# A list scheduler that orders the queues by another model of time

## Chip, cores and metric

One Trainium2 chip, one core. The metric is the device time of one execution in microseconds (us); below, a "run" is one such time, and a profile is one more execution taken with the hardware profiler.

## The reference, cut to what matters

The input `x` is 256 tokens by 1024 columns in float32 and passes through three layers. Layers 0 and 1 have a mixer, a cross-attention into 256 memory tokens and a gated feed-forward part; layer 2 has three mixers side by side, gates over them, and a gated feed-forward part with a short convolution.

```
for layer in range(2):
    y = mlstm_mixer(rms_norm(x, g[0])) if layer == 0 else stick_breaking_mixer(...)
    x = x + rms_norm(y, g[1])
    x = x + rms_norm(memory_cross_attention(rms_norm(x, g[2]), mem_n, ...), g[3])
    x = x + rms_norm(swiglu_ffn(rms_norm(x, g[4]), ...), g[5])
h = rms_norm(x); z = h @ w_in
merged = gate0 * (hgrn2(z) @ w_a) + gate1 * (fox(z) @ w_b) + gate2 * (memory(z) @ w_c)
x = x + merged @ w_out
x = x + conv_glu_ffn(rms_norm(x))
```

All weights are read once from HBM in float32: about 220 MB.

## The kernel before

**How the work is cut.** The tokens are two halves of 128 rows. Every large product splits both operands into a high and a low part of type `fp32r` and adds three products (high by high, high by low, low by high). A weight block of 128 rows x 1024 columns (512 KB) is loaded by a DMA on SP's queue (`load`, line 201), rounded to its high part on ScalarE (`split_weight`, line 209), and the low part is made on VectorE (line 210). Five buffers hold raw blocks, ten hold each of the split parts. The products are in `prod` (lines 238, 239 and 242, with up to 512 columns) and, where the result is wanted transposed, in `project_T` (lines 303 to 305, 256 columns). Two pools of four PSUM banks each take the results.

**The chains beside the products.** Between two stages stand chains of short operations. A norm is: squares summed on ScalarE (line 381), two tiny operations of GpSimd for the power -1/2 (`rstd`, lines 375 and 376), a scaling, transposes on TensorE (line 329), and splits on ScalarE and VectorE (lines 428 and 435). The first projection's chain scales by that factor on ScalarE (line 581) and copies after the transposes (line 356). The mixers have such chains too: attention, softmax and, in layer 2, the decay levels of `hgrn_levels` (lines 1147 to 1173; products at line 363) and the head norms (line 358).

**What sets the order.** Two programs order the work, one after the other.

1. While the kernel is traced, `Net` writes the instructions down in one order. The products are steps; a chain is a generator that yields the microseconds it is to wait, on a clock that advances with the products (0.2135 us for a 512-column product). The weights' loads and splits are written 24 and 14.85 us of that clock ahead of their product.
2. When the trace is closed, a list scheduler walks a model of the machine in time and puts the instructions into each engine's queue. Where an engine can take another instruction, it gets the one that stands earliest in the written order among those whose operands and buffers the model says are ready at that time. So the written order holds except where the model finds the next instruction not ready and a later one ready. Buffers are handed out in the same walk. On the chip each queue runs in the order so fixed and waits on semaphores.

```
def pe(self, us, main=False):          # the clock of the written order
    self.now += us
    if main: self.main += us; self.feed(); self.poll()
...
LEAD = 14.85
LEAD_DMA = 24.0
...
def ahead(self):
    return self.tc.high_priority(offset=60)
```

A few things the scheduler may not change: the first instructions of ScalarE, VectorE and TensorE are in a `manual_schedule` block (`start`), and table loads and some early transfers are pinned behind what was written before them on their engine (`keep_in_program_order`). All other transfers, the small constants and the gain rows (`gain`, line 215) may be moved.

## Time and profile before

| | |
|---|---|
| median of 3 runs | 1330.41 us (1330.31 to 1331.91) |
| profiled execution, its own time | 1330.58 us |
| its span, first to last instruction | 1328.9 us |
| around the span | 1.7 us |
| TensorE matmul busy | 1311.2 us, 8475 instructions |
| VectorE, ScalarE, GpSimd busy | 814.7, 693.1, 125.2 us |
| mean granted TensorE clock | 0.999 |

TensorE's busy time counts from a matmul's start to its modelled end, and neighbours overlap, so 99% busy does not by itself say that nothing can be gained between two products; what it does show is every stretch in which TensorE had no matmul at all. A wait is put down to the instruction whose semaphore came last.

### The profile page before, as it was taken

Reading aid. Unit: us, or ns where it says so; the run is one execution under the profiler, and the core shown is the slowest. Engines: PE = TensorE matmul, PEld = TensorE weight load, DVE = VectorE, ACT = ScalarE, POOL = GpSimd, SP = SyncE. Lnnn points to the kernel's source line nnn. Section 1 sums busy time; section 2 is a strip of 40 time slices with the busy share of each in tenths; the row PEclk is TensorE's granted clock in tenths of the full one; section 3 lists DMA queues with packets and bytes.
Section 4 is the critical chain, followed back from the end, with each engine's and each line's share of the span. In section 5 each row is a group of like instructions: output and inputs, shape, how many; then the busy total and the mean of one; then the engine's idle time right before and its main releaser. Section 6 shows DMA issues by size and latency. Waiting matters only on the chain.

```text
span 1328.9 us, 21515 instructions
## 1 busy us (share of the span) xinstructions
PE 1311.2 (99%) x8475; PEld 1180.9 (89%) x8475; DVE 814.7 (61%) x1229; ACT 693.1 (52%) x1128; POOL 125.2 (9%) x224
## 2 busy tenths in 40 slices
PE   8999999999999999999999999998999999999998
PEld 6889888899998999888889999888998999899997
DVE  6674576745446466468584454677786666766552
ACT  6864565534446577466474344555444534745441
POOL 3000000000001000016210000013224020000000
PEclk9999999999999999999999999999999999999999
DMA  7854562755556533554365655555244356456550
GB/s 254 288 185 133 160 205 84 235 173 170 183 187 204 193 128 127 190 182 139 110 219 167 211 181 179 182 170 163 72 140 127 128 160 207 152 180 197 181 178 32
DMA packets 121438, 224.47 MB, mean 169 GB/s; under 512 B 7448, under 2 KB 19066, under 8 KB 121338
## 3 DMA queue, kind: packets, MB, share of 16 engines
q1 hardware_dynamic: 121338, 223.11, 52.4%
q8 instruction: 66, 1.08, 0.3%
q14 instruction: 34, 0.28, 0.1%
HBM read 222.03 MB, written 1.05 MB: 168 GB/s over the span
## 4 chain that ended last, share of the span: by engine, by line
PE 78%; issue 14%; DVE 2%; POOL 2%; ACT 2%; DMA 1%; SPq 0%; DVEq 0%; POOLq 0%; ACTq 0%
PE mm L242 11%; PE mm L239 11%; PE mm L238 11%; PE tr L305 8%; PE tr L304 8%; PE tr L303 8%; PE tr L363 4%; PE mm L303 3%; PE mm L304 3%; PE mm L305 3%; PE tr L329 3%; PE tr L242 2%; PE tr L239 2%; PE tr L238 2%; DVE lo L210 1%
## 5 line engine op out<-in xcount | busy, mean ns | idle before, releaser
L210 DVE TENSOR_TENSOR lo<-raw,hi 128x1024 fp32r<-128x1024 f32 (+1 forms) x414 | 497.4, 1225 | 269.3 <-ACT hi L209 262.5
L209 ACT CAST hi<-raw 128x1024 fp32r<-128x1024 f32 (+1 forms) x414 | 419.6, 1042 | 202.5 <-PE mm L242 84.5
L238 PE MATMUL mm<-hi,t 128*128 128x512 f32 (+2 forms) x856 | 330.3, 387 | 0.0
L239 PE MATMUL mm<-lo,t 128*128 128x512 f32 (+2 forms) x856 | 327.6, 384 | 0.0
L242 PE MATMUL mm<-hi,t 128*128 128x512 f32 (+2 forms) x856 | 266.3, 386 | 0.0
L303 PE MATMUL tr<-t,hi 128*128 128x256 f32 x864 | 244.7, 283 | 0.0
L305 PE MATMUL tr<-t,lo 128*128 128x256 f32 x864 | 244.6, 283 | 0.0
L304 PE MATMUL tr<-t,hi 128*128 128x256 f32 x864 | 244.5, 283 | 0.0
L239 PEld LDWEIGHTS mm<-lo,t 128*128 128x128 f32 x856 | 161.6, 189 | 30.0
L238 PEld LDWEIGHTS mm<-hi,t 128*128 128x128 f32 x856 | 161.6, 189 | 29.2 <-issue 0.3
L242 PEld LDWEIGHTS mm<-hi,t 128*128 128x128 f32 x856 | 159.1, 189 | 30.2
L303 PEld LDWEIGHTS tr<-t,hi 128*128 128x128 f32 x864 | 165.8, 192 | 0.6
L304 PEld LDWEIGHTS tr<-t,hi 128*128 128x128 f32 x864 | 165.8, 192 | 0.6
L305 PEld LDWEIGHTS tr<-t,lo 128*128 128x128 f32 x864 | 165.8, 192 | 0.0
L303 PE MATMUL mm<-t,hi 128*128 128x256 f32 x576 | 165.7, 288 | 0.0
L304 PE MATMUL mm<-t,hi 128*128 128x256 f32 x576 | 163.0, 283 | 0.0
L305 PE MATMUL mm<-t,lo 128*128 128x256 f32 x576 | 163.0, 283 | 0.0
L303 PEld LDWEIGHTS mm<-t,hi 128*128 128x128 f32 x576 | 110.3, 191 | 2.0 <-issue 0.5
L304 PEld LDWEIGHTS mm<-t,hi 128*128 128x128 f32 x576 | 110.3, 192 | 0.8
L305 PEld LDWEIGHTS mm<-t,lo 128*128 128x128 f32 x576 | 110.2, 191 | 0.0
L375 POOL TENSOR_SCALAR s<-s 128x1 f32<-128x1 f32 x32 | 23.2, 726 | 798.2 <-ACT junk L381 787.1
L363 PE MATMUL tr<-t,t 128*128 128x128 f32 (+4 forms) x672 | 82.1, 292 | 2.9 <-DVE t L1155 2.9
(241 smaller groups left out, 1196.4 us busy)
## 6 DMA issues: line engine op xcount, KB each, us to landing
raw<-in_ffn_w_gate_up SPq DMA_DIRECT2D x88, 512.0 KB
raw<-in_ffn_w_down SPq DMA_DIRECT2D x66, 512.0 KB
raw<-in_w_in SPq DMA_DIRECT2D x54, 512.0 KB
raw<-in_ffn_w_up SPq DMA_DIRECT2D x44, 512.0 KB
raw<-in_xa_w_kv SPq DMA_DIRECT2D x32, 512.0 KB
raw<-in_sb_w_qkv SPq DMA_DIRECT2D x24, 512.0 KB
raw<-in_ml_w_in SPq DMA_DIRECT2D x22, 512.0 KB
raw<-in_xa_w_q SPq DMA_DIRECT2D x16, 512.0 KB
```

The lines of the kernel that those rows point to most:

```text
L209: self.nc.scalar.copy(hi, raw)
L210: self.nc.vector.tensor_sub(lo, raw, hi.bitcast(F32))
L238: nc.tensor.matmul(out, lhsT=a, rhs=wh, start=first and k == 0, stop=False)
L239: nc.tensor.matmul(out, lhsT=a, rhs=wl, start=False, stop=False)
L242: nc.tensor.matmul(out, lhsT=b, rhs=hl[k][0], start=False, stop=last and k == nk - 1)
L303: self.nc.tensor.matmul(out, lhsT=wh, rhs=xh, start=k == 0, stop=False)
L304: self.nc.tensor.matmul(out, lhsT=wh, rhs=xl, start=False, stop=False)
L305: self.nc.tensor.matmul(out, lhsT=wl, rhs=xh, start=False, stop=k == kt - 1)
L329: self.nc.tensor.transpose(ps[:, i * P : (i + 1) * P], src(i), self.ident)
L363: self.nc.tensor.matmul(out, lhsT=lhsT, rhs=rhs, start=start, stop=stop, **kw)
L375: nc.gpsimd.tensor_scalar(e, a, EPS, b, ALU.add, ALU.add)
```

## The change

Before the framework is imported, an environment variable is set that makes the list scheduler walk its second model of time, which keeps one timeline for each engine and queue, in place of its default model. Nothing else is changed: the written order, the instructions, the buffers and the pinned parts are the same. What can differ is the order in each queue, which buffer a tile gets, and with these the waits.

```
+import os
+os.environ["CONCOURSE_TILE_TIMELINE_SIM"] = "all"
 from collections import deque
 
 import concourse.bass as bass
```

## Rows read from the trace of the kernel before

**Rows 1.** The page: span, and busy time of each engine, share, instructions.

```profile
span 1328.9 us, 21515 instructions
...
PE 1311.2 (99%) x8475; PEld 1180.9 (89%) x8475; DVE 814.7 (61%) x1229; ACT 693.1 (52%) x1128; POOL 125.2 (9%) x224
```

**Rows 2.** Waits of TensorE: line waited for, total us, times, longest; ten rows.

```profile
PE tr L363 <- DVE t L1155: 2.9, 3, 1.5
PE tr L329 <- ACT t L581: 2.7, 1, 2.7
PE tr L329 <- DVE t L358: 2.6, 2, 1.7
PE tr L1565 <- DVE mhalf L490: 1.2, 1, 1.2
PE tr L329 <- DMA x<-in_x: 1.1, 1, 1.1
...
PE tr L329 <- DVE t L1221: 0.3, 1, 0.3
```

**Rows 3.** Timeline of the end: start us, us taken, engine, line, operation.

```profile
1323.74 0.39 PE L238 MATMUL mm<-hi,t 128*128 128x512 f32 x1
1323.97 0.39 PE L239 MATMUL mm<-lo,t 128*128 128x512 f32 x1
...
1324.20 0.61 PE L242 MATMUL mm<-hi,t 128*128 128x512 f32 x2
1324.85 0.75 DVE L1696 TENSOR_TENSOR x<-x,mm 128x256 f32<-128x256 f32 x2 [1.97 <-PE mm L242]
```

**Rows 4.** Timeline of the first chain; in brackets the wait and what ended it.

```profile
19.60 5.57 POOL L375 TENSOR_SCALAR s<-s 128x1 f32<-128x1 f32 x1 [15.59 <-ACT junk L381]
...
19.75 5.25 DVE L210 TENSOR_TENSOR lo<-raw,hi 128x1024 fp32r<-128x1024 f32 x5
...
25.85 0.69 ACT L581 ACTIVATE t<-mm,s 128x512 f32<-128x512 f32 x1 [2.71 <-POOL s L376]
...
26.59 0.66 PE L329 MATMUL tr<-ident,t 128*128 128x128 f32 x4 [2.66 <-ACT t L581]
```

**Rows 5.** Stretches: length, busy of PE, PEld, DVE, ACT, POOL, clock, DMA share, GB/s.

```profile
24.00:28.00 4.00, 1.41 (x9) 1.24 (x10) 1.00 (x2) 1.80 (x4) 2.58 (x4) 0.98 0.96 261
28.00:32.00 4.00, 4.00 (x14) 3.00 (x13) 3.88 (x8) 2.20 (x4) 0.00 (x0) 0.59 0.90 267
```

**Rows 6.** Timeline of TensorE in the mixers of layer 2.

```profile
928.97 0.41 PE L363 MATMUL tr<-t,t 128*128 128x64 f32 x2 [1.53 <-DVE t L1155]
929.18 0.37 PE L303 MATMUL mm<-t,hi 128*128 128x256 f32 x1
929.39 0.28 PE L304 MATMUL mm<-t,hi 128*128 128x256 f32 x1
```

**Rows 7.** That stretch, TensorE alone: length, busy, clock, DMA share, GB/s.

```profile
904.00:940.00 36.00, 29.63 (x228) 1.00 0.47 147
```

**Rows 8.** Waits of ScalarE, as in rows 2.

```profile
ACT hi L209 <- PE mm L242: 84.5, 95, 4.9
ACT hi L209 <- PE tr L304: 59.8, 29, 2.9
```

**Rows 9.** Waits of SP's queue, the one that issues the transfers, as in rows 2.

```profile
SPq L201 <- DVE lo L210: 987.6, 356, 22.8
```

**Rows 10.** Timeline of SP's queue: when two transfers were issued.

```profile
6.59 0.34 SPq L1387 DMA_DIRECT2D foxb<-in_fox_f_bias  x1
...
59.74 0.45 SPq L215 DMA_DIRECT2D g<-in_norm_gains  x1
```

**Rows 11.** Line 375 alone: duration min/median/max in ns, first and last start.

```profile
L375 POOL TENSOR_SCALAR s<-s x32: 293/378/5567, 19.6 to 1139.5; 128x1 f32<-128x1 f32 x32
```

**Rows 12.** Transfers: destination, source, queue, operation, count, size of each.

```profile
g<-in_norm_gains SPq DMA_DIRECT2D x6, 512.0 KB
```

## The prediction

> **What bounds the kernel now.** I read the page's busy times first. TensorE has a matmul in 1311.2 of 1328.9 us; VectorE, ScalarE and GpSimd are busy for 61%, 52% and 9% [rows 1]. No other engine is near being the bound, so what an order can change is TensorE's idle time, 1328.9 - 1311.2 = 17.7 us, and the pace of its products.
>
> The list of TensorE's waits comes next. Its ten rows add up to 13.3 us [rows 2]. The end adds 1328.9 - (1324.20 + 0.61) = 4.1 us after the last product, for the last sum and its way out [rows 3]. Together 17.4 of the 17.7 us. Of the 13.3, the waits for `mhalf` (1.2) and for `x` (1.1) lie in the pinned start; 13.3 - 2.3 = 11.0 us are waits that another order could move.
>
> They have two main places. In the first chain (timeline), GpSimd's line 375 began at 19.60 and took 5.57 us, while VectorE ran five splits of line 210 in 5.25 us; ScalarE then waited 2.71 us for the factor and TensorE 2.66 us for ScalarE [rows 4]. The stretches around show what such a wait leaves behind: TensorE was busy for 1.41 of the 4 us to 28, and in the next 4 us the granted clock was 0.59, between its two levels of 1.2 and 2.4 GHz [rows 5]. At full clock the work of those 4 us takes 4 x 0.59 = 2.4, so 1.6 us more were lost, and this late chain cost 2.7 + 1.6 = 4.3 us. The second place is the mixers of layer 2: 36 - 29.63 = 6.4 us without a matmul in 904 to 940 [rows 7]. There a level's small product waits 1.53 us for VectorE's line 1155, and gate products (lines 303 and 304) run right after it [rows 6]; they needed nothing that came in the meantime, so they could have gone first.
>
> The products themselves stand close: two of 512 columns start 0.23 us apart [rows 3]. The order of a queue doesn't change that pace, so nothing is taken from it.
>
> The waits of the other queues show what covers them. ScalarE stood at a split (line 209) 84.5 us in 95 waits and 59.8 in 29 until TensorE had freed a buffer, 4.9 us at the longest [rows 8]; SP's transfers waited 987.6 us for buffers [rows 9]. Weights are thus made as fast as TensorE uses them; outside the start neither transfers nor splits are short.
>
> **The change, part by part.** No instruction is added or taken away: the 1311.2 us of matmuls stay, and the variable itself is read on the host, at no device time. What moves is where the scheduler departs from the written order. That it does so freely today is seen on SP's queue: the bias `foxb`, written in layer 1 far behind the first stages, was issued at 6.59 us, and the first gain row of line 215 shown here at 59.74 [rows 10]. The trace doesn't show the second model's order, so I bound it from the rows.
>
> *Gains.* At most the 11.0 us of movable waits and the 1.6 us of low clock behind the first chain: 12.6 us, a time of 1318.0. At least nothing. I take half of the mixers' 6.4 us, 3.2: a model that keeps a timeline for each queue can find line 1155 late and take the gate products first, but then the chain's later steps stand behind whole groups of products. The middle is a choice between the two ends, since neither row is nearer.
>
> *Losses.* A stage entry is where products need the result of a chain: seven norm chains end in one (four behind the attention outputs, two behind layers 0 and 1's feed-forward part, one behind `w_out`). In the order of today TensorE's waits at all seven together are under 2 us (13.3 - 2.3 - 2.7 - 6.4 = 1.9). A chain that comes late there costs what the first chain cost, 4.3 us: nothing is queued behind the waiting transposes on TensorE that could run, and the splits of VectorE and ScalarE stop too when the buffers are full [rows 8]. Bounds: none late, 0; all seven, 30.1 us. How likely is one? Line 375 ran 32 times with a median of 378 ns and one of 5567 [rows 11]: 1 in 32 met a run of splits, and hurt. A new order moves the splits against all 32. I take two late chains, 8.6 us: nearer to today's one than to seven.
>
> The Trainium skill has a rule on this collision (SBUF — State Buffer, Who interferes with whom): a VectorE instruction with both inputs in SBUF and a GpSimd instruction that reads SBUF lock each other out, for the length of one instruction. Line 210 and line 375 are such a pair, and the row agrees that GpSimd waits. Where they differ is the length: one split of the row is 5.25 / 5 = 1.05 us, and the row shows a whole run of 5.57. By the row two late chains cost 8.6 us; by the rule 2 x 1.05 = 2.1, which is the rival "short collisions" below.
>
> *Nothing.* Table loads, constants and the end stay in the same number; ScalarE's idle half covers them [rows 1].
>
> Sum against the profiled execution's own time: 1330.6 (its span and 1.7 us around it) + 8.6 - 3.2 = 1336.0. The median of the runs is 1330.4, 0.2 us below, so the sum stands for the median as well.
>
> **The rivals.**
>
> *The mixers' waits go (faster).* The second model places the gate products in front of the late level products, and the chains stay in time: 1330.6 - 6.4 = 1324.2; with the first chain mended too, 1318.0 to 1320. For it: ready work stood right behind the waits [rows 6]. Against it: VectorE is the slow one there, and a level that is put off makes the next one late. It decides as long as fewer than two chains (8.6 us) turn late.
>
> *Short collisions, or nearly the same order (same).* The written order and the buffers are unchanged, and today's departures leave TensorE 13.3 us of waits in 8475 instructions. With two collisions of one split each: 1330.6 + 2.1 - 3.2 = 1329.5.
>
> *The variable isn't read (same).* The identical program, 1330.4. The queues would be the same instruction by instruction.
>
> *Transfers in front of the start (slower).* In 24 to 32 us DMA is busy for 0.96 and 0.90 of the time at 261 to 267 GB/s [rows 5]. A gain row of 512 KB [rows 12] takes 2.0 us of that. Both gain buffers filled there would hold the weights back 4.0 us, and with 1.6 us of low clock the time is 1336.2. Against it: SP waits mostly for buffers later on, and the memory's rows are pinned.
>
> *Chains behind waiting splits (much slower).* If the new order puts chain operations on ScalarE behind splits that wait for TensorE, each half of the seven entries can be late by the longest such wait, 4.9 us [rows 8]: 14 x 4.9 = 69 us, 1399. It decides only if the second model frees split buffers much earlier than the chip does.
>
> **How the numbers follow.** Likeliest, two or so late chains against half of the mixers' waits: 0.40, with a range of its own from 1333.3 to 1361. Mixers' waits go: 0.30. Short collisions or nearly the same order: 0.14. Not read: 0.04. Transfers in front: 0.06. Chains behind splits: 0.06. A measurement of this kernel can tell about 0.2%, 2.7 us, from no change. Slower by more: 0.40 + 0.06 + 0.06 = 0.52; within: 0.18; faster: 0.30. The time is the likeliest's, 1336. The range goes from the case in which all movable waits go, 1318, to the one with seven late chains, 1330.6 + 30.1 = 1361; it leaves out the 0.06 of 1399 and about as much again on either end.
>
> **What would show it.** Right: the same 8475 TensorE instructions and about 1311 us of products; TensorE's waits rise by some 5 us, in two or three new rows at transposes of line 329 or products behind a norm, each with a GpSimd line 375 of several us or a late ScalarE step ahead of it and a stretch with the clock under 1.00 after it; the stretch of the mixers loses about half of its 6.4 us. Wrong: TensorE's waits fall to the pinned start and little more (the faster rival); new waits of TensorE for weights in the first 50 us (transfers); the split's waits on ScalarE standing ahead of chain steps at every entry (much slower); or a changed pace of back-to-back products, which none of the cases holds.

## The result: 3.2% slower, and the profile after

The kernel with the second model takes 1374.19 us (median of 4 runs, 1372.44 to 1375.65) against 1330.63 us before on the same chip: ratio 1.0323, 95% interval 1.0310 to 1.0336. I had said 1336 us, at most 1361. The sign was right by luck: the mechanism that I had put into the sum is not the one that made the loss, and the size was not right either.

All line numbers of the kernel after are higher by 2 than those of before (line 329 is 331, line 375 is 377).

The page of the kernel after, to be read against [rows 1]:

```profile
span 1370.7 us, 21546 instructions
...
PE 1326.9 (97%) x8475; PEld 1191.0 (87%) x8475; DVE 812.3 (59%) x1229; ACT 695.0 (51%) x1131; POOL 121.2 (9%) x224
```

The same 8475 matmuls. TensorE is idle for 1370.7 - 1326.9 = 43.8 us in place of 17.7, which is 26.1 us of the 41.8 by which the span grew; the other 15.7 are matmuls that took longer. The mean granted clock, 0.991 in place of 0.999, accounts for most of these: 0.009 of 1370.7 us is about 12 us lost at the low level, against some 1 to 2 before. What made the rest of the 15.7, some 5 us, isn't traced here.

The instructions are not quite the same, though I had said so: ScalarE has 1131 in place of 1128. The three more are loads of a function table, 17 in place of 14, of 1.28 us each, and all three stand between 42 and 60 us. What such loads can do is seen in the last of the experiments.

TensorE's waits after, to be read against [rows 2] (line waited for, total us, times, longest):

```profile
PE tr L999 <- DVE t L993: 4.6, 3, 2.4
PE tr L331 <- ACT t L792: 3.9, 1, 3.9
PE tr L240 <- ACT t L430: 3.1, 4, 1.8
...
PE tr L331 <- DVE t L1223: 2.9, 1, 2.9
PE tr L331 <- DVE t L775: 2.7, 2, 1.7
PE mm L305 <- DVE t L1223: 2.4, 1, 2.4
PE tr L999 <- DVE t L994: 2.4, 1, 2.4
```

There is no single big wait. The head of the list holds steps of quite different chains (attention, head norm, gates), each a few us. Where do they stand? The order of TensorE's queue differs from before's only inside stretches: between them both queues have issued the same set of instructions, so the n-th large product (lines 238 to 242 and 303 to 305) can be compared in the two traces. Nearly all of the loss lies in three stretches (39.4 of the 41.8 us). They are, with the same work, 155.0 to 251.0 us (before 158.5 to 243.7: the cross-attention of layer 0), 470.7 to 573.8 (before 463.0 to 550.9: the stick-breaking attention), and 606.1 to 689.5 (before 583.0 to 653.0: the head norm behind that attention, and what follows). The windows of after, TensorE alone (length, busy, clock, DMA share, GB/s):

```profile
155.00:251.00 96.00, 87.02 (x442) 1.00 0.43 143
470.70:573.80 103.10, 95.03 (x712) 0.97 0.39 124
606.10:689.50 83.40, 73.04 (x366) 0.94 0.42 137
```

and of before:

```profile
158.50:243.70 85.20, 85.20 (x440) 1.00 0.50 161
463.00:550.90 87.90, 87.90 (x713) 1.00 0.43 138
583.00:653.00 70.00, 68.55 (x369) 1.00 0.51 159
```

The same number of matmuls to within three. Before, TensorE was idle for 0, 0 and 1.45 us there; after, for 8.98, 8.07 and 10.36. The three stretches grew by 10.8 + 15.2 + 13.4 = 39.4 us, of which 26.0 are idle time. These stages had next to no wait in the list of before, and I had not looked inside them.

Two stretches answer to rows that I had used. In the first chain, GpSimd's line 377 now takes 1.01 and 1.82 us where it took 5.57 [rows 4], and TensorE is busy without a gap where it was busy for 1.41 of 4 us [rows 5]. The timeline of GpSimd and the windows:

```profile
20.13 1.01 POOL L377 TENSOR_SCALAR s<-s 128x1 f32<-128x1 f32 x1 [16.09 <-ACT junk L383]
...
23.78 1.82 POOL L377 TENSOR_SCALAR s<-s 128x1 f32<-128x1 f32 x1 [2.00 <-ACT junk L383]
```

```profile
24.00:28.00 4.00, 4.00 (x19) 3.30 (x19) 2.91 (x5) 2.05 (x4) 2.15 (x2) 1.00 0.84 199
28.00:32.00 4.00, 4.00 (x21) 3.31 (x20) 1.32 (x2) 2.40 (x3) 0.00 (x0) 1.00 1.03 376
```

So the head is some 4 us ahead of before. And of the mixers' waits for line 1155 [rows 6] none is left, but others stand there (2.4 us for line 1223, 2.1 for line 770), and the stretch of layer 2 that took 63 us, from 901 to 964, takes 64:

```profile
938.00:1002.00 64.00, 58.68 (x458) 0.95 0.38 119
```

It has 5.3 us without a matmul in place of 6.4, but the clock of 0.95 takes 0.05 x 64 = 3.2 us back.

The longest line 377 in the whole kernel is the 1.82 us in the head, and the next is 1.60 us, at 235.84, where the same norm had 1.44 before; this row answers to [rows 11]:

```profile
L377 POOL TENSOR_SCALAR s<-s x32: 296/298/1817, 20.1 to 1178.8; 128x1 f32<-128x1 f32 x32
```

My two late chains, each with a GpSimd operation of several us ahead of it, don't exist.

What a lost chain looks like now, in the stick-breaking attention: ScalarE's queue, then VectorE's, then TensorE's (start, us taken, engine, line; in brackets the wait and what ended it).

```profile
531.31 0.63 ACT L989 ACTIVATE t<-t 128x512 f32<-128x512 f32 x1
...
534.84 1.05 ACT L211 CAST hi<-raw 128x1024 fp32r<-128x1024 f32 x1 [2.90 <-PE mm L306]
...
535.79 0.63 ACT L990 ACTIVATE t<-t 128x512 f32<-128x512 f32 x1
536.33 2.93 ACT L211 CAST hi<-raw 128x1024 fp32r<-128x1024 f32 x3
539.16 0.59 ACT L988 ACTIVATE t<-tr 128x512 f32<-128x512 f32 x1
```

```profile
538.79 0.42 DVE L993 CAST t<-t 128x512 fp32r<-128x512 f32 x1
539.13 2.35 DVE L212 TENSOR_TENSOR lo<-raw,hi 128x1024 fp32r<-128x1024 f32 x2
541.40 0.69 DVE L994 TENSOR_TENSOR t<-t,t 128x512 fp32r<-128x512 f32 x1
```

```profile
542.14 0.59 PE L999 MATMUL tr<-t,nle 128*128 128x512 f32 x1 [2.38 <-DVE t L994]
543.20 0.80 PE L999 MATMUL tr<-t,nle 128*128 128x512 f32 x1 [0.47 <-DVE t L993]
543.79 0.63 PE L240 MATMUL mm<-hi,t 128*128 128x512 f32 x1
544.22 0.63 PE L241 MATMUL mm<-lo,t 128*128 128x512 f32 x1
```

Line 990 could have followed line 989 at 531.94. In ScalarE's queue a weight split stands ahead of it, which waits 2.90 us for TensorE to free a buffer; three more splits stand ahead of the next step, 2.93 us. On VectorE two more, 2.35 us, stand between the chain's lines 993 and 994, and line 994 is what TensorE's wait of 2.38 us is for. TensorE's queue has come to the steps that this chain feeds: it waits, and the products after the wait start 0.43 us apart (the granted clock is 0.50 from 543.6 to 545.6 us), where products at full clock start 0.23 apart [rows 3].

In before, four such groups (there lines 986 to 988) run in a row from 503.13 to 510.49 with no split between their steps, and the split that waits for TensorE comes after them:

```profile
509.86 0.63 ACT L988 ACTIVATE t<-t 128x512 f32<-128x512 f32 x1
512.77 3.18 ACT L209 CAST hi<-raw 128x1024 fp32r<-128x1024 f32 x3 [2.28 <-PE mm L304]
```

What TensorE's own queue does to a chain shows in a number worked out from trace and program together: for each of the 384 transposes of line 329, the time from the end of the last instruction that wrote its operand to its own start. The median is 1.58 us before and 3.18 us after. A ready transpose stands behind some 1.6 us more of products. The 908 short instructions of chains on TensorE stand, at the median, behind 15 more large products than before. The Trainium skill (PSUM — Partial Sum Buffer, Engine vs sequencer instructions) says that matmuls start and complete in program order and that the queues of ScalarE, VectorE and GpSimd are strictly first in, first out; the trace agrees: ready transposes stood 3.18 us behind products at the median, and ready steps of ScalarE behind a split that waited 2.90 us.

### The profile page after: what moved, and what is told of

The parts are those of the page before. It is cut to its first block, busy times and chain, and to the rows that moved or that the text cites. A ratio compares the mean times of both kernels' runs of the same rounds, so it can differ in the third digit from the quotient of the medians.

```text
span 1370.7 us, 21546 instructions
## 1 busy us (share of the span) xinstructions
PE 1326.9 (97%) x8475; PEld 1191.0 (87%) x8475; DVE 812.3 (59%) x1229; ACT 695.0 (51%) x1131; POOL 121.2 (9%) x224
## 3 DMA queue, kind: packets, MB, share of 16 engines
HBM read 222.03 MB, written 1.05 MB: 163 GB/s over the span
## 4 chain that ended last, share of the span: by engine, by line
PE 86%; issue 5%; DVE 3%; ACT 3%; POOL 1%; DMA 1%; SPq 0%; DVEq 0%; ACTq 0%; POOLq 0%
PE mm L240 12%; PE mm L241 12%; PE mm L244 12%; PE tr L307 8%; PE tr L306 8%; PE tr L305 8%; PE mm L305 5%; PE mm L307 5%; PE mm L306 5%; PE tr L365 4%; PE tr L331 2%; PE tr L244 2%; PE tr L240 2%; PE tr L241 1%; DVE lo L212 1%
## 5 line engine op out<-in xcount | busy, mean ns | idle before, releaser
L365 PE MATMUL tr<-t,t 128*128 128x128 f32 (+4 forms) x672 | 87.2, 298 | 7.1 <-DVE t L779 3.0
L377 POOL TENSOR_SCALAR s<-s 128x1 f32<-128x1 f32 x32 | 16.5, 517 | 827.7 <-ACT junk L383 811.5
```

Of the source, the lines that this page charges most:

```text
L365: self.nc.tensor.matmul(out, lhsT=lhsT, rhs=rhs, start=start, stop=stop, **kw)
L377: nc.gpsimd.tensor_scalar(e, a, EPS, b, ALU.add, ALU.add)
```

## The experiments

Two things were needed: a queue's order without the model that made it, and the other way round. Both come from one function. It puts an edge without a wait between neighbours of a list, so that the scheduler, with either model, keeps that queue in that order. The queues that a run doesn't name are ordered anew around the pinned ones, so a run with one queue pinned does not change that queue alone:

```
     with tile.TileContext(nc) as tc:
         build(tc, aps, out)
+        pin(nc, tc)
...
+    for engine, text in ORDER.items():
...
+        for a, b in zip(order, order[1:]):
+            tc.add_manual_dep(b, a.name, info, reason="pin")
```

The theories: **A**, TensorE's order makes the loss; **B**, the orders of ScalarE and VectorE (splits ahead of chain steps) make it; **C**, the second model's choice of buffers and transfers makes it. Where it is set against C, the sum of A and B (the order of the queues, whichever) is called **Q**. All kernels below do the same computation as before.

### One queue at a time

Second model, with TensorE's queue held to before's order: `ORDER` has the key `PE`, from before.

> The second model schedules everything, but TensorE's queue is fixed instruction by instruction to the order of the kernel before. Theory A (the loss sits in TensorE's order: products overtake each other and the transposes): back to 1328 to 1342 us, TensorE's waits under 20 us. Theory B (it sits in the order of ScalarE and VectorE: splits stand in front of chain steps): stays at 1360 or more. Theory C (it sits in the buffers that the second model hands out): stays at 1360 or more as well.

Second model, ScalarE's queue of before (`Activation`):

> The second model, with ScalarE's queue alone fixed to the order of the kernel before. Theory A: 1365 to 1380 us, the places of the three losses unchanged. Theory B: 1330 to 1350, because no split that waits for TensorE stands in front of a chain step any more. Theory C: about 1374.

Second model, VectorE's queue of before (`DVE`):

> The second model, with VectorE's queue alone fixed to the order of the kernel before. Theory A: 1365 to 1380 us. Theory B, if VectorE's part of it counts: 1330 to 1360. Theory C: about 1374.

The counterpart: default model, TensorE's queue of after.

> The default model schedules everything, but TensorE's queue is fixed to the order that the second model gave it. Theory A: 1360 to 1385 us, as slow as the changed kernel. Theory B and theory C: 1328 to 1340, since ScalarE, VectorE and the buffers follow the default model.

Measured: 1361.82 us (ratio 1.0228, 1.0213 to 1.0243), 1366.5 (1.0262, 1.0247 to 1.0277), 1376.04 (1.0328, 1.0311 to 1.0345) and 1372.92 (1.0313, 1.0297 to 1.0328). TensorE's order of after is enough: under the default model, with the other queues as that model orders them around it, it costs all of it. Mending it is not enough: with TensorE's order of before the second model still loses 30 us. None of the three queues tried heals more than 12.4 us by itself. Theory A's forecasts hold in three of the four runs, and the one on mending TensorE's queue, 1328 to 1342, is missed by 20 us: it holds in one direction only. Theory B's forecasts for ScalarE's and VectorE's queues are both missed, and C by itself can't be, since the fourth run has the loss without the second model.

What remains in the first of these kernels, ScalarE's queue in the stick-breaking attention:

```profile
522.89 1.05 ACT L209 CAST hi<-raw 128x1024 fp32r<-128x1024 f32 x1 [4.08 <-PE mm L304]
523.84 0.59 ACT L986 ACTIVATE t<-tr 128x512 f32<-128x512 f32 x1
524.33 1.05 ACT L209 CAST hi<-raw 128x1024 fp32r<-128x1024 f32 x1
525.27 0.64 ACT L987 ACTIVATE t<-t 128x512 f32<-128x512 f32 x1
525.80 1.04 ACT L209 CAST hi<-raw 128x1024 fp32r<-128x1024 f32 x1
526.74 0.63 ACT L988 ACTIVATE t<-t 128x512 f32<-128x512 f32 x1
```

A split that waits 4.08 us for TensorE, then a split between any two steps of the chain. Twice in this attention TensorE waits 3.35 us for such a chain (line 997 for VectorE's line 991, at 489.53 and, behind the steps shown, at 530.23).

### Several queues

Second model, four queues of before, which leaves it the order of SP's queue and the buffers; then TensorE's and ScalarE's; then these two and GpSimd's.

> The second model schedules, but the queues of TensorE, ScalarE, VectorE and GpSimd are held to before's order; only SP's queue and the choice of buffers are left to it. If the loss sits in the order of the engines' queues (theory Q), this gives before's time again, 1331 to 1334 us, although TensorE's queue alone gave 1361.8 and ScalarE's alone 1366.5: the losses would be shared by queues that wait for one another. If the second model's buffers or transfers cost something of their own (theory C), part of the 43 us stays: 1340 or more.

> The second model with TensorE's and ScalarE's queues of before; VectorE, GpSimd and SP as the model orders them. TensorE's alone gave 1361.8, ScalarE's alone 1366.5, four queues 1331.7. If the rest of the loss sits in splits ahead of chain steps on ScalarE, 1332 to 1340. If VectorE and GpSimd hold a share as large (constants and subtractions ahead of chain steps), 1341 to 1358.

> The second model with the queues of TensorE, ScalarE and GpSimd of before; VectorE's and SP's as the model orders them. With TensorE's and ScalarE's alone it was 1346.6 us, 7.9 us of its loss at the border to the second layer, where the wait for line 1221 on VectorE (4.5 us) stands. If GpSimd's constants ahead of the norm's operations make that loss, it goes: 1336 to 1341. If VectorE's order makes it, 1345 to 1348.

Measured: 1331.71 us (ratio 1.0001, 0.9991 to 1.0010), 1346.62 (1.0120, 1.0106 to 1.0134) and 1342.98 (1.0092, 1.0078 to 1.0106). With four queues of before the loss is gone within the interval, about 1 us either way. The second model did choose otherwise there: a gain row that before issued at 59.74 us [rows 10] went out at 33.50, ahead of nine loads of weights. So theory C is out: its buffers and transfers cost nothing that can be measured while the four queues are held, and the whole loss is the order of these four. GpSimd's share was forecast to bring 1336 to 1341, or nothing; measured is 1342.98, between the two forecasts, a share of 3.6 us. What is left to VectorE, 1.0092 against 1.0001 or some 12 us, is the larger one, although VectorE's order alone gave nothing back. The shares depend on what else is mended.

GpSimd's part can be seen. Its queue in the head norm behind the stick-breaking attention, with TensorE's and ScalarE's queues of before:

```profile
645.40 0.25 POOL L1219 TENSOR_SCALAR s<-s 128x4 f32<-128x4 f32 x1
...
646.20 0.82 POOL L483 TENSOR_SCALAR_AFFINE_SELECT t<-t 128x64 f32<-128x64 f32 x4
...
647.36 0.23 POOL L373 TENSOR_SCALAR s<-s 128x4 f32<-128x4 f32 x1
...
650.06 0.24 POOL L1220 TENSOR_SCALAR s<-s 128x4 f32<-128x4 f32 x1
```

and with GpSimd's of before as well:

```profile
644.49 0.25 POOL L1219 TENSOR_SCALAR s<-s 128x4 f32<-128x4 f32 x1 [2.80 <-DVE s L1218]
...
646.28 0.24 POOL L1220 TENSOR_SCALAR s<-s 128x4 f32<-128x4 f32 x1
```

Constants for layer 2 (lines 483, 1093 and 1100), needed much later, stand between the four operations of the norm, which take 4.90 us from first to last in place of 2.03. TensorE's wait for line 1221 is 4.5 us in the one and 0.3 in the other.

### The two halves of TensorE's order

TensorE's order of after was taken apart: 7176 large products and 908 short steps of chains. Theory **D**: the steps stand too late behind products. Theory **E**: the order of the products among themselves. Default model, only TensorE's queue pinned.

> Default model; TensorE's queue only is written out: the 7176 large products in before's order among themselves, and each of the 908 chain steps (transposes, column sums, scan products) behind as many products as stood in front of it after the change, which is 24 products later on the mean. If the loss comes from chain steps that stand behind products taken ahead (theory D), this is as slow as the whole of TensorE's order of after under the default model, 1372.9 us: 1365 to 1380. If it comes from the order of the products among themselves (theory E), it is near before: 1328 to 1338.

> The counterpart: default model; TensorE's products in after's order among themselves, each chain step behind as many products as in front of it before the change. Theory D: near before, 1327 to 1340. Theory E: 1365 to 1380. Both halves in the middle, near 1350, would say that each has a share.

> Default model and before's order of products; every chain step on TensorE is put 8 products later than before (7.1 on the mean where data allow it), which is 1.5 us at 0.213 us a product, about the additional wait of a ready transpose behind products that the trace of after shows (median 1.58 to 3.18 us). Theory D, if the delay alone is enough: a loss at the stages with chains and few products, 10 to 30 us: 1341 to 1361. If a delay of this size is hidden by the products, 1331 to 1335.

Measured: 1390.3 us (1.0437, 1.0421 to 1.0452), 1363.95 (1.0234, 1.0217 to 1.0251) and 1349.32 (1.0138, 1.0118 to 1.0158). Late steps with before's products lose more than the whole order of after, and more than the 1380 that theory D allowed. A delay of 8 products on TensorE, 7.1 on the mean or 1.5 us, costs 17.6 us, with the other queues ordered around it: it is not hidden. But theory E isn't empty: its run was neither near before, as theory D had it, nor in theory E's 1365 to 1380, but 1.05 us below. The place of the losses tells more than the sums. The last two rows of the table belong to the next section, and the three rows above them to runs told above. The table says how much later than in before the next product starts at the end of each stretch, less the same at its beginning (us; stretches by the time of before; worked out from the starts of the products in the traces):

```
                                  0-72  72-117 117-244 244-463 463-552 552-654 654-834 834-1002 1002-1324
after                             -3.3     0.0    10.3     0.7    15.4    13.4     0.9      1.6      3.1
TensorE's order of after           3.9     0.3     6.6     0.5    13.8    12.6     0.4      1.3      3.2
late chain steps only              4.9     0.6    10.8     2.6    14.1    16.8     2.9      1.6      3.2
product order only                 0.3     0.0    14.7     0.0     0.0    11.2    -0.1      8.0      0.0
steps 8 late                      -2.4     0.5     1.6     0.9     5.5     7.8     1.0      0.4      2.5
TensorE's order of before         -2.2     2.3     2.0     1.4    13.1     9.8     0.9      1.4      3.1
TensorE's and ScalarE's of before -0.1     0.6     2.1     1.5     0.0     8.5     0.9      1.3      0.8
these two and GpSimd's            -0.0     0.6     2.2     1.4     0.0     2.8     1.0      1.4      1.2
window 16                         -2.9     0.0     5.1     0.5     9.2    10.5    -0.3     -3.3      1.1
window 4                          -3.7     0.0    -0.6     0.0     3.1     8.4    -0.5     -0.5      0.5
```

In the stick-breaking attention (463 to 552) the product order costs nothing and the late steps cost 14.1 of after's 15.4: theory D. There ScalarE's splits cost 13.1 too in the row with TensorE's order of before, and 0.0 once ScalarE's is of before as well: either delay is enough, and they don't add up. Behind it (552 to 654) the late steps cost 16.8 and the product order 11.2; of the latter, 8.9 lie between 552 and 602, where after loses nothing, so it is a loss of the experiment's own making, from steps held at places that the new order of products had outrun. In the cross-attention (117 to 244) each half alone costs as much as after loses, and the two cannot be told apart.

The median wait of a ready transpose of line 329 goes along where the steps were moved: 1.58 us before, 2.14 with steps 8 late, 2.80 with the late steps, 3.18 after. With the product order only it is 1.47, less than before, and yet 32 us are lost: this number does not measure theory E's share. And the late steps, slower than after, have the shorter wait.

### The model's window

Why does the second model put them late? It has a parameter for how many instructions TensorE's sequencer may hold in front of the array, 35 as it stands. A step that gets ready after that many products have been handed over can only come behind them. If so, the loss must shrink with that number; this is the model's parameter, and no run here measures the chip's own. Two orders were made with it cut, and all five queues held to them:

```
+TRN2Spec.ENG_ISSUE_QUEUE_DEPTH[mybir.EngineType.PE] = 16
```

> The second model with one parameter cut: the number of instructions that it lets TensorE's sequencer hold in front of the array, 16 in place of 35. All five queues are held to the order that the model then gives: a chain step stands 7 products later than before at the median (15 in after). Theory D (the model commits products ahead of chain steps that become ready a little later) asks for a loss between nothing and after's 43 us that falls with the window: 1342 to 1362. If the window has no part in it, 1366 or more.

> The same with 4 in place of 35: a chain step stands 1 product later than before at the median, and the total displacement of TensorE's queue against the written order is 30,922 places (67,024 in after, 11,428 in before). Theory D: 1331 to 1345. A theory that blames some other part of the second model (its durations, its one timeline per queue) expects most of the loss to stay, 1355 or more.

Measured: 1350.47 us (1.0148, 1.0135 to 1.0162) with 16 and 1336.59 (1.0044, 1.0029 to 1.0059) with 4. From 35 to 16 to 4 the loss falls from 43.6 to 19.5 to 5.6 us, and the median wait of a ready transpose from 3.18 to 2.11 to 1.44 us. Of the 5.6 that stay, the table has 8.4 at the head norm, with GpSimd's constants still between its operations (lines 483, 1093 and 1100 again, 4.91 us from 645.29 on), and a gain of 3.7 in the head. Waits of TensorE with a window of 4:

```profile
PE tr L329 <- DVE t L1221: 4.3, 1, 4.3
PE tr L363 <- DVE t L777: 3.1, 1, 3.1
PE mm L303 <- DVE s L1238: 2.4, 1, 2.4
```

### A version that beats both

After is ahead of before at two places, the head and for a while the mixers. First TensorE's order alone was taken there, then all queues that differ; the rest is before's order, under the default model.

> A try for a kernel faster than both. Default model; TensorE's queue is before's but for three stretches, in which it is the order of another run that was ahead there: places 58 to 196 (the head, after: 4.6 us ahead of before) and 852 to 909 (1.8 us) from after, 5398 to 5699 (the mixers, 7.2 us in the run with ScalarE's order of before) from that run. If what TensorE's order gains at a place is its own, the sum is 8 to 13 us less than before: 1318 to 1324. If it hung on the other queues, 1328 to 1336.

> Default model, all five queues held to before's order but for two stretches. In the first 36 us they have the order of the run with a window of 4 (4.2 us ahead there, 0.5 us given back by 70 us); in the mixers, 905 to 1000 us, TensorE and VectorE have the order of the run with ScalarE's queue of before (7.2 us ahead at 959 us, 3 us given back after). If these gains are the order of the queues together, 1331.0 less 7 to 10: 1321 to 1324. If they hung on what went before, or come back later as in the run with TensorE's order alone, 1328 to 1335.

> The same head; in the mixers, 905 to 966 us, TensorE, VectorE and ScalarE have the order of the run with a window of 16 (5.1 us ahead, 2.1 us given back). Gains kept: 1331.0 less 5 to 8: 1323 to 1326. Gains lost: 1328 to 1335.

Measured: 1333.97 us (1.0022, 1.0013 to 1.0031), 1323.39 (0.9949, 0.9935 to 0.9962) and 1325.19 (0.9961, 0.9949 to 0.9974). TensorE's order alone was 3.9 us ahead at 48 us and 2.1 behind at 72. The other queues were ordered anew around it, and ScalarE's shows what that cost: line 609 got in between the pinned load of a function table and lines 631 and 632, which share it, and the kernel has 18 table loads in place of 14. The first two lines are of this run, the other two of before:

```profile
52.79 1.28 ACT L631 ACT_TABLE_LOAD   x1
...
54.31 1.28 ACT L632 ACT_TABLE_LOAD   x1
```

```profile
53.06 0.20 ACT L631 ACTIVATE s<-s 128x4 f32<-128x4 f32 x1
53.29 0.21 ACT L632 ACTIVATE s<-s 128x4 f32<-128x4 f32 x1
```

TensorE then waits 2.8 us for VectorE's lines 635 and 640, which follow line 632. The runs with TensorE's order of after and with late steps only have 18 loads as well, and lose 3.9 and 4.9 us up to 72 in the table; after has 17, and all other runs 14. No run changes the loads alone, so their share is not shown. With the queues together the gains stay, 3.3 us in the head and 4.5 or 3.3 in the mixers. The page of the faster one, and the first of its waits of TensorE:

```profile
span 1321.3 us, 21508 instructions
...
PE 1309.3 (99%) x8475; PEld 1179.3 (89%) x8475; DVE 812.1 (61%) x1229; ACT 693.0 (52%) x1128; POOL 127.2 (10%) x224
```

```profile
PE tr L1565 <- DVE mhalf L490: 1.2, 1, 1.2
PE mm L303 <- ACT t L1150: 1.2, 1, 1.2
```

Idle time of TensorE is 12.0 us, against 17.7 in before [rows 1].

## Why the prediction was wrong, point by point

- **What bounds the kernel**: right. TensorE is the bound before and after, with the same 8475 matmuls, and the loss is idle time and the low clock behind it.
- **Gains** (3.2 us in the mixers): not there. The waits for line 1155 went, others came, 1.1 us of idle time were saved, and the low clock behind the new waits took more than that: the stretch took 1.0 us longer, and 1.6 from 834 to 1002. The gain that did come is the first chain, which I had named as movable and left out of the sum: 4.6 us by 48 us, 3.3 kept at 72. Its price of 4.3 us was about right.
- **Losses** (8.6 us, two late norm chains): this is the step that failed. I priced a late chain by the one example that the trace of before held, a collision of GpSimd's line 375 with a run of splits, and counted the entries at which it might happen again. It happened at none of them with that length: the longest line 377 of after is 1.82 us and stands in the head, the next 1.60. Nor was the row of before "1 in 32": at 173.11 and 232.99 line 375 took 1.43 and 1.44 us beside splits, and TensorE lost nothing there. The loss came from the order itself, in which a chain's steps stand behind products on TensorE, behind splits on ScalarE and VectorE, and behind constants on GpSimd, 39.4 us in three stretches. I had counted the ends of norm chains alone and put the steps inside an attention or a head norm at nothing; TensorE's waits there were nearly nothing [rows 2], but that said how well before's order fed them, not how much slack they had. A delay of 8 products a step, 1.5 us of products on the mean, costs 17.6 us.
- ***Chains behind waiting splits***, the rival with a chance of 0.06 and 1399 us, was the nearest. Its mechanism is seen (2.90 and 4.08 us at splits ahead of chain steps), and its condition, that the model frees split buffers much earlier than the chip, wasn't tested. But it is one of four shares: ScalarE's queue of before gives back 8 us alone. The prediction's own signs had named "a late ScalarE step" as well, without a price.
- **Short collisions, transfers in front, variable not read**: none. Transfers are out by the run with four queues held, 1331.71 us, and the head came out ahead. That table loads "stay in the same number" was wrong, 17 for 14.
- **The bounds.** Seven late chains at 4.3 us made 30.1 and the end of the range. I bounded by norm chains only; the attention's chain, with three operations on ScalarE and three on VectorE between two steps on TensorE, lost most (15.4 us).

## What to carry to other kernels

A list scheduler that commits instructions to a deep queue ahead of the engine puts products in front of short steps that get ready a moment later. With TensorE full, that costs nothing at the step and everything at the end of the chain, where the products run out: look at stages with few products and long chains, even if they have no wait today, and ask how much later their steps may come. Compare two orders stretch by stretch, between places at which both queues have issued the same set, and take the better one for all queues together; one queue of a good order in an order made for others can lose what it promised. Count the loads of ScalarE's function tables as well: an order that lets another function in between adds some, and here 14 became 17 or 18.

## What the runs showed of the hardware

Line 377 of after, which began at 23.78 and ended at 25.60, ran beside four splits of VectorE from 21.92 to 25.52; it ended 0.08 us after the last of them:

```profile
21.92 3.60 DVE L212 TENSOR_TENSOR lo<-raw,hi 128x1024 fp32r<-128x1024 f32 x4
```

As in [rows 4], where line 375 ended 0.17 us after its run of five, GpSimd came through at the end of the run of splits, not after one of them. By the Trainium skill (SBUF — State Buffer, Who interferes with whom) two such operations contend, and the lock is exclusive; that it is held for a whole instruction stands there of the modes that take both ports. Read so for splits too, the rule gives 0.90 and 1.05 us, a quarter of a run of 3.60 and a fifth of one of 5.25; the rows show 1.82 and 5.57, and the measurement decides. Behind a single split the two agree: at 232.99 in before line 375 ended 0.07 us after the one split of VectorE that ran there, from 233.14 to 234.36.

That a loss from four queues can be whole with one of them alone (1372.92 us with TensorE's order, under the default model) and just as whole with another mended (1376.04 with VectorE's), I had not expected: the shares of queues that feed one another can't be summed.
